# One-core decoder block: 128x128 transposes by TensorE, or 32x32 blocks by VectorE with DMA between the block positions

## The chip, the cores and the metric

The kernel runs on one core of a Trainium2 chip. A core has TensorE (PE, matmuls; PEld is its weight load), VectorE (DVE), ScalarE (ACT), GpSimd (POOL) and SyncE (SP, which here issues almost all DMAs). The metric is device microseconds of one execution, as the median of several runs. The numbers of single instructions come from one profiled execution.

## The reference, cut to what matters

One layer of a decoder, 256 tokens by 2048 channels, all in float32:

```python
h = rms_norm(x, mix_norm_g)
p = h @ w_in                      # split into the inputs of three head groups
y_lru = rg_lru_branch(...)        # 512 channels
y_ml  = mlstm_branch(...)         # 768 channels; the last step is  h * norm_g * silu(z)
y_mo  = moba_branch(...)          # 768 channels; the last step is  o * silu(z)
x = x + concat([y_lru, y_ml, y_mo]) @ w_out
hx, hm = rms_norm(x, xa_norm_g), rms_norm(mem, mem_norm_g)
q = hx @ wq;  k, v = split(hm @ wkv)          # 4 heads of 128, 256 memory tokens
x = x + (softmax(q @ k.T * s) @ v) @ wo
return rms_norm(x, final_norm_g)
```

A matmul on TensorE contracts over the partitions. What stands with tokens on the partitions (a gated branch, the residual, the probabilities) has to be turned, so that channels (or memory tokens) stand on the partitions, before it can be contracted over them.

## The kernel before, in words

All weights are streamed from memory in 172 chunks, and each float32 operand is cut into a high and a low part, so that a product is three matmuls. The chunks are numbered in the order of use. Those that matter here: z1 is 92 to 99, z2 is 100 to 107, out0 to out3 (the output projection, four groups of 512 columns) are 108 to 139 in eights, ck0, ck2, cq0, cq2 are 140 to 155 in fours, cv is 156 to 163 and wo0 to wo3 are 164 to 171.

The order on every engine is written out by hand (manual schedule): each engine runs its instructions strictly in the order in which the program emits them. The loop over chunks `i` (L1100 to L1124) emits, in this order: `split(i + 4)`, which makes the high part of chunk `i + 4` on ACT (L197) and its low part on DVE (L198, through the helper at L148); `load(i + 8)` on SP's queue (L172), which waits until the raw buffer of chunk `i + 4` is free, that is, until DVE has made its low part, since there are 4 raw buffers; `mm(i)`, the matmuls of chunk `i` on PE; and then one `step()`. There are 6 pairs of high and low buffers, so `split(i + 4)` also waits for the matmuls of chunk `i - 2`.

`step()` runs the generator at the head of a queue of side work up to its next `yield`. I call the call of `step()` after `mm(i)` "step i". `done(name, a)` puts work on the queue when a group of columns is complete. For the stretch that the change touches, the steps of the kernel before are:

- step 99: `gate_z` of z1; steps 100 to 102: the last of `mo_heads`, which writes `o` (buffer w1); step 103: `ml_y` multiplies `hh` by its gate; steps 104, 105, 106: it turns pairs of 128 channels by `to_channels` (four PE transposes into one PSUM bank, L739) and cuts them into high and low parts, the operands y2, y3, y4 (L754, L755).
- step 107: `gate_z` of z2; step 108: `mo_y(0, 1)` multiplies; step 109: it turns and makes y5 (`split_pair`, ACT at L239, DVE at L240); step 110: `mo_y(1, 3)` multiplies; steps 111 and 112: y6 and y7.
- out0 reads y0 in chunk 108, y1 in chunk 109 and so on to y7 in chunk 115. The operands y0 and y1 come from another branch, much earlier.
- `x1_evac(a, g)` at the end of each out group adds the residual (step 115, 123, 131, 139) and turns the sum in two steps after it (L858), which gives h0 to h7, the operands of cq0 and cq2. Between them lie `x1_load` (the residual, L843) and `mem_stats` (loads of the transposed memory, L222, and their squares on ACT, L401).
- step 155 to 159: `cq_evac(a, 2)`: queries, scores and softmax for two tiles of 128 tokens, then for each tile eight PE transposes of the probabilities (L916) and two ACT copies (L917) into `C["pT"]`. After chunk 163 `cv_out` copies the values out of PSUM on ACT and DVE (L926, L927) and multiplies them with `C["pT"]` (L932, L937); the wo chunks follow.

Buffers of the pool `wk` are named by tag (`big(5, ...)` is tag w5) and there is one of each: a new tile of a tag waits until all readers of the old one are done.

Of the kernel before, what the change touches and what calls it, by code (L numbers as in the profile page):

```python
# [105 lines left out]
def kernel(ctx: ExitStack, tc: tile.TileContext, xT, memT, x, mem, ws, vec_d, lw_d, fg_d, out):  # L106
    nc = tc.nc
# [19 lines left out]
    def ps():  # L127
        nps[0] += 1
        return psp.tile([128, 512], F32, tag="ps", name=f"ps{nps[0]}")
# [77 lines left out]
    def act_pair(which, j):  # L207

        a = acts.tile([128, 2, 2, 256], F32R, tag="y" if which in "ym" else "x", name=f"a_{which}{j}")
        act_all[which][j] = a  # L210
        act_hi[which][j], act_lo[which][j] = a[:, :, 0, :], a[:, :, 1, :]
        return act_hi[which][j], act_lo[which][j]
# [518 lines left out]
                S.activation(dst[:, t, d0:d0 + c1 - c0], a[t][:, c0:c1], AF.Silu, scale=rstd["x"][:, t:t + 1])  # L731
        yield

    def to_channels(src, c):

        p = ps()
        for cc in range(2):
            for t in range(2):
                P.transpose(p[:, cc * 256 + t * 128:cc * 256 + t * 128 + 128],  # L739
                            src[:, t, (c + cc) * 128:(c + cc) * 128 + 128], ident)  # L740
        return p

    def ml_y():
        hh, sz = M["h"], M["sz"]
        for t in range(2):
            tt(hh[:, t, :], hh[:, t, :], sz[:, t, :], OP.mult)
        yield
        for j in range(3):
            p = to_channels(hh, 2 * j)
            h, l = act_pair("y", 2 + j)  # L750
            for cc in range(2):
                sl = slice(cc * 256, cc * 256 + 256)
                ng = vc("ng", 2 * j + cc)
                S.activation(h[:, cc, :], p[:, sl], AF.Copy, scale=ng)  # L754
                stt(l[:, cc, :], p[:, sl], ng, h[:, cc, :].bitcast(F32), OP.mult, OP.subtract)  # L755
            yield


    B = {}
# [67 lines left out]
    def mo_y(j0, j1):  # L827
        o, sl = B["o"], slice(256 * j0, 256 * j1)
        for t in range(2):
            tt(o[:, t, sl], o[:, t, sl], B["sz"][:, t, sl], OP.mult)  # L830
        yield
        for j in range(j0, j1):
            split_pair("y", 5 + j, to_channels(o, 2 * j))
            yield


    X1 = {}
# [9 lines left out]
    def x1_evac(a, g):  # L847
        t1 = X1[g]
        for t in range(2):
            tt(t1[:, t, :], a[t], t1[:, t, :], OP.add)  # L850
            junk = small("yt", 512)
            S.activation(junk, t1[:, t, :], AF.Square, accum_out=ssq1[:, t, g:g + 1])
        yield
        for j in range(2):
            p = ps()
            for kk in range(2):
                for t in range(2):
                    P.transpose(p[:, kk * 256 + t * 128:kk * 256 + t * 128 + 128],  # L858
                                t1[:, t, (2 * j + kk) * 128:(2 * j + kk) * 128 + 128], ident)
            split_pair("h", 2 * g + j, p)  # L860
            yield

    def x1_rstd():
        r = small("rstd_1", 2)
# [14 lines left out]
    def cq_evac(a, c):  # L879
        if c == 0:  # L880
            C["q"] = big(2, 4, 256)
        qT = C["q"]
        fold(qT[:, c:c + 2, :], a)
        if c == 0:
            yield
            return
        sc, nsc = small("ca_sc", 2), small("ca_nsc", 2)
        V.tensor_scalar(sc, rstd["1"], DH_SCALE, None, op0=OP.mult)
        V.tensor_scalar(nsc, rstd["1"], -DH_SCALE, None, op0=OP.mult)
        yield  # L890
        pr = [big(6, 4, 256), big(9, 4, 256)]
        for t in range(2):
            mx, sm_ = small(f"ca_mx{t}", 4), small(f"ca_sm{t}", 4)
            for hp in range(2):
                p = ps()
                for hh_ in range(2):
                    h = 2 * hp + hh_
                    P.matmul(p[:, hh_ * 256:hh_ * 256 + 256], qT[:, h, t * 128:t * 128 + 128], C["k"][:, h, :],
                             start=True, stop=True)
                V.reduce_max(mx[:, 2 * hp:2 * hp + 2], p.rearrange("p (a b) -> p a b", a=2), axis=AX.X)  # L900
                V.tensor_scalar(mx[:, 2 * hp:2 * hp + 2], mx[:, 2 * hp:2 * hp + 2], nsc[:, t:t + 1], None, op0=OP.mult)
                for hh_ in range(2):
                    h = 2 * hp + hh_
                    S.activation(pr[t][:, h, :], p[:, hh_ * 256:hh_ * 256 + 256], AF.Exp, scale=sc[:, t:t + 1],
                                 bias=mx[:, h:h + 1], accum_out=sm_[:, h:h + 1])
            V.reciprocal(sm_, sm_)
            for h in range(4):
                V.tensor_scalar(pr[t][:, h, :], pr[t][:, h, :], sm_[:, h:h + 1], None, op0=OP.mult)
            yield
        C["pT"] = [big(2, 4, 2, 128), big(5, 4, 2, 128)]  # L910
        for t in range(2):
            for hp in range(2):
                p = ps()
                for i in range(4):
                    h, m = 2 * hp + i // 2, i % 2
                    P.transpose(p[:, i * 128:i * 128 + 128], pr[t][:, h, m * 128:m * 128 + 128], ident)  # L916
                S.activation(C["pT"][t][:, 2 * hp:2 * hp + 2, :, :].rearrange("p a b c -> p (a b c)"), p, AF.Copy)  # L917
            yield

    def c_pair(t):  # L920
# [1 line left out]
        return a[:, 0, :, :], a[:, 1, :, :]  # L922

    def cv_out(a):
        v = [wk.tile([128, 512], F32, tag=f"w{i}", name=f"cv{i}") for i in (6, 1)]
        S.activation(v[0], a[0], AF.Copy, scale=rstd["m"][:, 0:1])  # L926
        V.tensor_scalar(v[1], a[1], rstd["m"][:, 1:2], None, op0=OP.mult)  # L927
        C["oh"], C["ol"] = [], []
        pv = [ps(), ps()]
        for t in range(2):  # L930
            for h in range(4):
                P.matmul(pv[t][:, h * 128:h * 128 + 128], v[0][:, h * 128:h * 128 + 128], C["pT"][t][:, h, 0, :],  # L932
                         start=h == 0, stop=False, skip_group_check=True)
        for t in range(2):
            p = pv[t]
            for h in range(4):
                P.matmul(p[:, h * 128:h * 128 + 128], v[1][:, h * 128:h * 128 + 128], C["pT"][t][:, h, 1, :],  # L937
                         start=False, stop=True, skip_group_check=True)
            oh, ol = (v.rearrange("p a b -> p (a b)") for v in c_pair(t))
            S.activation(oh, p, AF.Copy)  # L940
            tt(ol, p, oh.bitcast(F32), OP.subtract)
            C["oh"].append(oh)
            C["ol"].append(ol)
# [50 lines left out]


    queue = deque()

    def bg(*gens):
        queue.extend(gens)
# [6 lines left out]

    def step(n=1):

        while queue and n > 0:
            try:  # L1010
                if next(queue[0]):
                    return
                n -= 1
            except StopIteration:
                queue.popleft()

    def drain():
        while queue:
            step()

    def idle(n):
# [173 lines left out]
```

## Time and profile before

| | |
|---|---|
| time, median of 3 runs | 522.26 us (521.66 to 522.65) |
| the profiled execution, its time | 521.88 us |
| the profiled execution, its span | 520.2 us |
| PE busy | 507.9 us |
| DVE busy | 338.0 us |
| ACT busy | 292.8 us |
| DMA moved | 98.74 MB, mean 190 GB/s |

The span is what the profile shows between the first and the last instruction; the 1.7 us between span and time lie around it. "Busy" is the time in which an engine has an instruction in work; issuing a DMA is not counted as busy. A wait in the trace is named after what ended it.

### The profile page before, as it was taken

The numbers are of one execution on the slowest core, as the hardware profiler recorded it, in microseconds if no ns is written. First come the engines' busy times: TensorE is split into PE (matmuls) and PEld (weight loads), VectorE is DVE, ScalarE is ACT, GpSimd is POOL, SyncE is SP. The second block draws the span as 40 slices with busy tenths as digits, with TensorE's granted clock in tenths as the row PEclk, the third lists the DMA queues.
The fourth block names the chain that finished last, engine by engine and source line by source line (L and its number), as shares of the span: only waits on it lengthen the run. The fifth ranks groups of instructions, "written<-read, shape, count | busy, mean of one in ns | idle before, by whom it ended". The sixth has DMA issues, their size and how long they took to land.

```text
span 520.2 us, 7578 instructions
## 1 busy us (share of the span) xinstructions
PE 507.9 (98%) x2814; PEld 448.8 (86%) x2814; DVE 338.0 (65%) x531; ACT 292.8 (56%) x476; POOL 54.8 (11%) x70
## 2 busy tenths in 40 slices
PE   8999999999999999999999999999999999999993
PEld 6999889998988888889988888888888888888883
DVE  5958848895397656548645466654658749637574
ACT  5775477678544333353545755543649467546353
POOL 2800001000132100002000000000132003000000
PEclk9999999999999999999999999999999999999998
DMA  8995635467446544435843465478575527734704
GB/s 274 360 412 180 187 120 167 139 221 230 160 160 178 186 161 163 151 92 183 271 155 121 137 209 179 164 272 325 188 264 174 194 66 259 237 128 129 234 3 161
DMA packets 31077, 98.74 MB, mean 190 GB/s; under 512 B 3520, under 2 KB 3904, under 8 KB 31040
## 3 DMA queue, kind: packets, MB, share of 16 engines
q1 hardware_dynamic: 30896, 98.25, 56.9%
q8 instruction: 22, 0.36, 0.3%
q14 instruction: 15, 0.12, 0.1%
q10 hardware_dynamic: 144, 0.01, 0.0%
HBM read 96.15 MB, written 2.10 MB: 189 GB/s over the span
## 4 chain that ended last, share of the span: by engine, by line
PE 85%; issue 6%; POOL 3%; DVE 3%; DMA 1%; ACT 1%; SPq 1%; POOLq 0%; ACTq 0%; DVEq 0%
PE acc_out L284 5%; PE acc_out L282 5%; PE acc_out L283 5%; PE acc_q L260 4%; PE acc_k L260 4%; PE acc_z L284 4%; PE acc_z L282 4%; PE acc_z L283 4%; PE acc_cq L260 3%; PE acc_lz L260 3%; PE acc_q L261 2%; PE acc_k L261 2%; PE acc_o L283 2%; PE acc_o L282 2%; PE acc_o L284 2%
## 5 line engine op out<-in xcount | busy, mean ns | idle before, releaser
L148 DVE TENSOR_TENSOR wl<-raw,wh 128x1024 fp32r<-128x1024 f32 (+3 forms) x166 | 199.6, 1212 | 111.7 <-ACT wh L197 109.3
L197 ACT ACTIVATE wh<-raw 128x1024 fp32r<-128x1024 f32 (+2 forms) x162 | 161.8, 1013 | 44.5 <-DMA raw<-ws 14.8
L282 PE MATMUL acc_out<-wh,a_y 128*128 128x512 f32 x128 | 50.8, 397 | 0.0
L284 PE MATMUL acc_out<-wh,a_y 128*128 128x512 f32 x128 | 49.9, 390 | 0.0
L283 PE MATMUL acc_out<-wl,a_y 128*128 128x512 f32 x128 | 49.8, 389 | 0.0
L282 PE MATMUL acc_z<-wh,a_x 128*128 128x512 f32 x96 | 39.6, 412 | 0.0
L284 PE MATMUL acc_z<-wh,a_x 128*128 128x512 f32 x96 | 37.6, 391 | 0.0
L283 PE MATMUL acc_z<-wl,a_x 128*128 128x512 f32 x96 | 37.5, 390 | 0.0
L260 PE MATMUL acc_k<-a_x,wh 128*128 128x512 f32 x96 | 34.4, 401 | 0.0
L260 PE MATMUL acc_q<-a_x,wh 128*128 128x512 f32 x96 | 34.1, 398 | 0.0
L451 POOL TENSOR_TENSOR w<-ev,rrow 128x512 f32<-128x512 f32 x11 | 17.5, 1589 | 153.6 <-DVE ev L148 153.6
L284 PEld LDWEIGHTS acc_out<-wh,a_y 128*128 128x128 f32 x128 | 24.0, 188 | 5.2
L283 PEld LDWEIGHTS acc_out<-wl,a_y 128*128 128x128 f32 x128 | 24.1, 188 | 4.7
L282 PEld LDWEIGHTS acc_out<-wh,a_y 128*128 128x128 f32 x128 | 24.1, 188 | 4.6
L261 PE MATMUL acc_k<-a_x,wl 128*128 128x256 f32 x96 | 26.9, 280 | 0.0
L261 PE MATMUL acc_q<-a_x,wl 128*128 128x256 f32 x96 | 26.8, 280 | 0.0
L402 POOL TENSOR_TENSOR mask<-mask,yt 128x512 f32<-128x512 f32 x7 | 10.3, 1473 | 147.1 <-ACT yt L401 147.1
L260 PE MATMUL acc_lz<-a_x,wh 128*128 128x512 f32 x64 | 23.3, 406 | 0.0
L260 PE MATMUL acc_ck<-a_m,wh 128*128 128x512 f32 x64 | 23.1, 403 | 0.0
L260 PE MATMUL acc_cq<-a_h,wh 128*128 128x512 f32 x64 | 22.7, 399 | 0.0
L283 PE MATMUL acc_o<-wl,a_x 128*128 128x392 f32 (+1 forms) x64 | 21.6, 338 | 0.0
L282 PE MATMUL acc_o<-wh,a_x 128*128 128x392 f32 (+1 forms) x64 | 21.6, 337 | 0.0
(302 smaller groups left out, 1187.4 us busy)
## 6 DMA issues: line engine op xcount, KB each, us to landing
raw<-ws SPq DMA_DIRECT2D x138, 512.0 KB, 4.1
raw<-ws SPq DMA_DIRECT2D x24, 384.0 KB, 3.1
w<-x SPq DMA_DIRECT2D x8, 512.0 KB, 6.5
raw<-ws SPq DMA_DIRECT2D x8, 392.0 KB, 3.1
w<-memT SPq DMA_DIRECT2D x8, 256.0 KB, 6.1
out<-xg SPq DMA_DIRECT2D x8, 256.0 KB, 3.0
w<-xT SPq DMA_DIRECT2D x7, 256.0 KB, 6.7
raw<-ws SPq DMA_DIRECT2D x4, 256.0 KB, 5.0
```

The costliest lines, as they stand in the source:

```text
L148: V.tensor_tensor(out, a, b, op)
L197: S.activation(h[:, :kc * n], r[:, :kc * n], AF.Copy)
L260: P.matmul(a[m], h[:, sl], both, start=first, stop=False, skip_group_check=True)
L261: P.matmul(a[m][:, :256], l[:, sl], xh, start=False, stop=last, skip_group_check=True)
L282: P.matmul(o, xh[:, sl], mh, start=first, stop=False)
L283: P.matmul(o, xh[:, sl], ml, start=False, stop=False)
L284: P.matmul(o, xl[:, sl], mh, start=False, stop=last)
L402: G.tensor_tensor(sq[which], sq[which], q, OP.add)
L451: G.tensor_tensor(dst, e, rb(which), OP.mult)
```

## The change

Three places that turned 128x128 tiles on PE now do it in two moves: one DVE instruction transposes every 32x32 block in place of its position (into a buffer `tmp`), and 16 DMAs from SBUF to SBUF carry block (i, j) to position (j, i) for all tiles at once. Each of the 16 DMAs has 32 partitions and one piece of 32 floats (128 bytes) per tile. `turn` is called nine times: for `ml_y` (12 tiles), `mo_y` (4 tiles, then 8), `x1_evac` (8 tiles, four times) and the probabilities (8 tiles, twice). What read the turned PSUM bank is put into a generator `finish` on a list `side`; every `step()` advances all of `side` first, and `finish` lets 4, 2 or 3 steps pass (`idle`) before it reads. ACT's copies at L917 are gone. In `cv_out` the first buffer of the values is now w2 in place of w6.

```diff
-    def to_channels(src, c):
-        p = ps()
-        for cc in range(2):
-            for t in range(2):
-                P.transpose(p[:, cc * 256 + t * 128:cc * 256 + t * 128 + 128],
-                            src[:, t, (c + cc) * 128:(c + cc) * 128 + 128], ident)
-        return p
+    def turn(dst, tmp, src):
+        V.transpose(tmp, src)
+        for i in range(4):
+            for j in range(4):
+                nc.sync.dma_start(dst[32 * j:32 * j + 32, :, 32 * i:32 * i + 32],
+                                  tmp[32 * i:32 * i + 32, :, 32 * j:32 * j + 32])
+
+    def blocks(t, c0, c1):
+        return t[:, :, c0 * 128:c1 * 128].rearrange("p t (c k) -> p c t k", k=128)

     def ml_y():
...
-        for j in range(3):
-            p = to_channels(hh, 2 * j)
-            h, l = act_pair("y", 2 + j)
...
+        tmp, hT = big(8, 6, 2, 128), big(4, 6, 2, 128)
+        turn(hT.rearrange("p a b c -> p (a b) c"), tmp.rearrange("p a b c -> p (a b) c"), blocks(hh, 0, 6))
+        def finish():
+            yield from idle(4)
+            for j in range(3):
+                h, l = act_pair("y", 2 + j)
...
+                yield
+        side.append(finish())
+        yield
...
     def mo_y(j0, j1):
...
-        yield
-        for j in range(j0, j1):
-            split_pair("y", 5 + j, to_channels(o, 2 * j))
-            yield
+        if j0 == 0:
+            B["tmp"], B["oT"] = big(5, 6, 2, 128), big(9, 6, 2, 128)
+        oT = B["oT"]
+        cs = slice(2 * j0, 2 * j1)
+        turn(oT[:, cs]..., B["tmp"][:, cs]..., blocks(o, 2 * j0, 2 * j1))
+        def finish():
+            yield from idle(2)
+            for j in range(j0, j1):
+                split_pair("y", 5 + j, oT[:, 2 * j:2 * j + 2].rearrange("p a b c -> p (a b c)"))
+                if j < 2:
+                    yield
+        side.append(finish())
+        yield
...
     def x1_evac(a, g):
...
-                    P.transpose(...)
-            split_pair("h", 2 * g + j, p)
-            yield
+        tmp, xT1 = big(1, 4, 2, 128), big(2, 4, 2, 128)
+        turn(xT1..., tmp..., blocks(t1, 0, 4))
+        def finish():
+            yield from idle(3)
+            for j in range(2):
+                split_pair("h", 2 * g + j, xT1[:, 2 * j:2 * j + 2].rearrange("p a b c -> p (a b c)"))
+                yield
+        side.append(finish())
+        yield
...
     def cq_evac(a, c):
...
-        C["pT"] = [big(2, 4, 2, 128), big(5, 4, 2, 128)]
-        for t in range(2):
-            for hp in range(2):
-                p = ps()
-                for i in range(4):
-                    h, m = 2 * hp + i // 2, i % 2
-                    P.transpose(p[:, i * 128:i * 128 + 128], pr[t][:, h, m * 128:m * 128 + 128], ident)
-                S.activation(C["pT"][t][:, 2 * hp:2 * hp + 2, :, :].rearrange("p a b c -> p (a b c)"), p, AF.Copy)
+        C["pT"] = []
+        for t in range(2):
+            tmp, pT = big(1 + t, 8, 128), big(5 + t, 8, 128)
+            turn(pT, tmp, pr[t].rearrange("p h (m k) -> p (h m) k", k=128))
+            C["pT"].append(pT.rearrange("p (h m) k -> p h m k", m=2))
             yield
...
     def cv_out(a):
-        v = [wk.tile([128, 512], F32, tag=f"w{i}", name=f"cv{i}") for i in (6, 1)]
+        v = [wk.tile([128, 512], F32, tag=f"w{i}", name=f"cv{i}") for i in (2, 1)]
...
     def step(n=1):
+        for g in list(side):
+            if next(g, True):
+                side.remove(g)
         while queue and n > 0:
...
     def drain():
-        while queue:
+        while queue or side:
             step()
```

## Rows read from the trace of the kernel before

**Rows 1.** The page, part 1: busy us (share of the span) xinstructions.
```profile
PE 507.9 (98%) x2814; PEld 448.8 (86%) x2814; DVE 338.0 (65%) x531; ACT 292.8 (56%) x476; POOL 54.8 (11%) x70
```
**Rows 2.** Busy time by stretch: bounds, length, PE, PEld, DVE, ACT, POOL; clock, DMA, GB/s.
```profile
294.00:320.00 26.00, 26.00 (x133) 21.87 (x132) 16.40 (x18) 18.02 (x32) 0.00 (x0) 1.00 0.55 182
```
**Rows 3.** Chain of waits: start us, us, what; the three kinds of transpose groups.
```profile
309.82 0.43 PE ps L739 x4
...
345.34 0.44 PE ps L858 x4
...
470.68 0.87 PE ps L916 x8
```
**Rows 4.** Timeline of SP's queue at the start: start us, us to issue, line, DMA.
```profile
1.23 0.42 SPq L169 DMA_DIRECT2D raw<-ws  x1
1.70 0.42 SPq L222 DMA_DIRECT2D w<-xT  x1
...
5.50 0.65 SPq L222 DMA_DIRECT2D w<-xT  x1
6.75 0.33 SPq L172 DMA_DIRECT2D raw<-ws  x1
```
**Rows 5.** DMA from 0 to 14 us: a queue's packets, MB, share; issues, us to landing.
```profile
q10 hardware_dynamic: 144, 0.01, 0.7%
...
w<-xT SPq DMA_DIRECT2D x2, 128.0 KB, 2.6
...
vec<-vec ACTq DMA_DIRECT2D x1, 8.0 KB, 2.2
```
**Rows 6.** Timeline of DVE, 300 to 350 us: start us, us, line, operation, out<-in [idle before].
```profile
308.88 1.22 DVE L148 TENSOR_TENSOR wl<-raw,wh 128x1024 fp32r<-128x1024 f32 x1
310.81 0.48 DVE L151 SCALAR_TENSOR_TENSOR a_y<-ps,vec,a_y 128x256 fp32r<-128x256 f32 x1 [0.71 <-ACT a_y L754]
...
325.93 0.69 DVE L148 TENSOR_TENSOR a_y<-ps,a_y 128x512 fp32r<-128x512 f32 x1 [1.65 <-ACT a_y L239]
...
328.02 1.29 DVE L148 TENSOR_TENSOR w<-w,w 128x512 f32<-128x512 f32 x2
```
**Rows 7.** Timeline of ACT, 300 to 350 us.
```profile
319.02 1.26 ACT L731 ACTIVATE w<-acc_z,rstd_x 128x512 f32<-128x512 f32 x2
320.16 2.01 ACT L197 ACTIVATE wh<-raw 128x1024 fp32r<-128x1024 f32 x2
325.30 0.60 ACT L239 ACTIVATE a_y<-ps 128x512 fp32r<-128x512 f32 x1 [3.13 <-PE ps L739]
```
**Rows 8.** Timeline of PE: first matmuls of chunks 108, 109 and 110 (out0).
```profile
319.22 0.39 PE L282 MATMUL acc_out<-wh,a_y 128*128 128x512 f32 x1
...
321.94 0.39 PE L282 MATMUL acc_out<-wh,a_y 128*128 128x512 f32 x1
...
325.02 0.48 PE L282 MATMUL acc_out<-wh,a_y 128*128 128x512 f32 x1
```
**Rows 9.** Waits of the whole span: who waited for whom, us in total, times, longest.
```profile
ACT yt L852 <- PE ps L433: 9.2, 1, 9.2
PE acc_ck L261 <- DVE wl L148: 0.8, 1, 0.8
```
**Rows 10.** Timeline of DVE at the softmax of the cross-attention.
```profile
462.64 0.69 DVE L900 TENSOR_REDUCE ca_mx<-ps 128x2 f32<-128x512 f32 x1 [1.06 <-PE ps L898]
...
474.35 1.22 DVE L148 TENSOR_TENSOR wl<-raw,wh 128x1024 fp32r<-128x1024 f32 x1
```
**Rows 11.** Timeline of ACT, at the copy of the values.
```profile
484.78 0.69 ACT L926 ACTIVATE cv<-acc_cv,rstd_m 128x512 f32<-128x512 f32 x1 [2.07 <-PE acc_cv L293]
```
**Rows 12.** Timeline of PE, probabilities times values.
```profile
485.94 1.95 PE L932 MATMUL ps<-w,cv 128*128 128x128 f32 x16
```
**Rows 13.** Busy time by stretch, as rows 2, around the last matmul.
```profile
511.00:512.00 1.00, 0.95 (x8) 0.74 (x7) 0.44 (x2) 0.51 (x2) 0.00 (x0) 1.00 0.00 0
516.00:517.00 1.00, 0.00 (x0) 0.00 (x0) 0.00 (x0) 0.00 (x0) 0.00 (x0) 0.67 1.09 342
```

More of the change, by code (lines that the diff above doesn't have):

```diff
@@ L747, in ml_y @@
         yield
-        for j in range(3):
-            p = to_channels(hh, 2 * j)
-            h, l = act_pair("y", 2 + j)
[L751 to L755, printed above, removed]
-            yield
+        tmp, hT = big(8, 6, 2, 128), big(4, 6, 2, 128)
[4 more added lines that the diff above has]
+                h, l = act_pair("y", 2 + j)
+                for cc in range(2):
+                    src = hT[:, 2 * j + cc, :, :].rearrange("p a b -> p (a b)")
+                    ng = vc("ng", 2 * j + cc)
+                    S.activation(h[:, cc, :], src, AF.Copy, scale=ng)
+                    stt(l[:, cc, :], src, ng, h[:, cc, :].bitcast(F32), OP.mult, OP.subtract)
+                yield
+        side.append(finish())
+        yield
     B = {}
@@ L830, in mo_y @@
             tt(o[:, t, sl], o[:, t, sl], B["sz"][:, t, sl], OP.mult)
+        if j0 == 0:
+            B["tmp"], B["oT"] = big(5, 6, 2, 128), big(9, 6, 2, 128)
+        oT = B["oT"]
+        cs = slice(2 * j0, 2 * j1)
+        turn(oT[:, cs].rearrange("p a b c -> p (a b) c"), B["tmp"][:, cs].rearrange("p a b c -> p (a b) c"),
+             blocks(o, 2 * j0, 2 * j1))
+        def finish():
[5 more added lines that the diff above has]
+        side.append(finish())
         yield
-        for j in range(j0, j1):
-            split_pair("y", 5 + j, to_channels(o, 2 * j))
-            yield
     X1 = {}
@@ L853, in x1_evac @@
         yield
-        for j in range(2):
-            p = ps()
-            for kk in range(2):
-                for t in range(2):
-                    P.transpose(p[:, kk * 256 + t * 128:kk * 256 + t * 128 + 128],
-                                t1[:, t, (2 * j + kk) * 128:(2 * j + kk) * 128 + 128], ident)
-            split_pair("h", 2 * g + j, p)
-            yield
+        tmp, xT1 = big(1, 4, 2, 128), big(2, 4, 2, 128)
+        turn(xT1.rearrange("p a b c -> p (a b) c"), tmp.rearrange("p a b c -> p (a b) c"), blocks(t1, 0, 4))
+        def finish():
[5 more added lines that the diff above has]
+        yield
     def x1_rstd():
@@ L909, in cq_evac @@
             yield
-        C["pT"] = [big(2, 4, 2, 128), big(5, 4, 2, 128)]
+        C["pT"] = []
         for t in range(2):
-            for hp in range(2):
-                p = ps()
-                for i in range(4):
-                    h, m = 2 * hp + i // 2, i % 2
-                    P.transpose(p[:, i * 128:i * 128 + 128], pr[t][:, h, m * 128:m * 128 + 128], ident)
-                S.activation(C["pT"][t][:, 2 * hp:2 * hp + 2, :, :].rearrange("p a b c -> p (a b c)"), p, AF.Copy)
+            tmp, pT = big(1 + t, 8, 128), big(5 + t, 8, 128)
+            turn(pT, tmp, pr[t].rearrange("p h (m k) -> p (h m) k", k=128))
+            C["pT"].append(pT.rearrange("p (h m) k -> p h m k", m=2))
             yield
@@ L996 @@
     queue = deque()
+    side = []
     def bg(*gens):
```

## The prediction

> **What bounds the kernel now.** I read the busy times first: PE is busy for 507.9 us of a span of 520.2 us, DVE and ACT for about two thirds and just over half of it [rows 1]. An average says little about a stage, so the stretch in which the change begins comes next: PE is busy for all of its 26 us [rows 2]. The chain of waits says the same from the other side: the PE transposes lie on it, 0.43 to 0.44 us for a group of four and 0.87 us for a group of eight [rows 3]. So PE's own instructions are the time, and whatever PE no longer does is saved in full, as long as nothing makes PE wait. SP issues a DMA every 0.47 us when it has several in a row (0.42 us each and a small gap [rows 4]); this interval, s below, decides the case.
>
> **What is removed.** There are 14 groups of four transposes (six at L739, eight at L858) and two groups of eight at L916: 14 x 0.44 + 2 x 0.87 = 7.9 us of PE [rows 3]. ACT's copies at L917 were off the path and count as nothing. A second, smaller gain: in the kernel before, ACT waits 9.2 us for a PE matmul of the memory statistics, and PE then loses 0.8 us for a low part in ck0 [rows 9]. The side list lets the queue move sooner, the statistics end in out2 (steps 129 and 130), and this wait should go: 0.8 us. Together -8.7 us.
>
> **What is added.** No row shows a DVE block transpose. The nearest are one-input and two-input DVE operations: 0.69 us for 512 elements per partition [rows 10], 1.22 us for 1024 [rows 6]; the line through them gives 1.8 us for 1536. I take these (at half the rate the times would double, which adds 1 to 2 us in each place below). The nine turns issue 144 DMAs on SP. For s, 0.47 us is the value at back-to-back issue; the ends are 0.33 us, the shortest issue, and 0.65 us, one that was held by an earlier DMA [rows 4]. The time from issue to landing is 2.2 to 2.6 us for the smallest transfers [rows 5]; I take 2.4 us.
>
> A DMA of the 12-tile turn moves 32 x 12 pieces of 128 bytes, 24 for each of 16 DMA engines. The nearest row is a queue of 144 packets, nearly all of 64 bytes, with 0.7% of 14 us x 16 engines: 11 ns each [rows 5]. At 11 ns per piece that is 0.26 us, at 22 ns (twice the bytes) 0.53 us; for 8 tiles 0.18 or 0.35 us. So the issue, not the movement, sets the pace: 16 x 0.47 = 7.5 us for a turn.
>
> The Trainium skill, "DMA: Bandwidth & Descriptors", section "Specifications", speaks against such pieces: below 512 bytes a transfer misses line rate, because of a read-modify-write. Its section "Why small descriptors are slow (HBM only)" exempts transfers inside SBUF. By the first the pieces would take about twice as long (the second rival below), by the second the sum here stands; no row of this trace shows an SBUF to SBUF transfer.
>
> **First place: y2 and y5 at out0.** All times are those of the trace before. The 12-tile turn is in step 104, behind the low part of chunk 108 on DVE, which ends at 310.1 [rows 6]; the transpose ends at 311.9. SP then issues 16 DMAs until 319.4, after that the load of chunk 113 (until 319.9), which stood behind them, and then the 16 DMAs of the 4-tile turn, which now comes in step 105: until 327.4, landed at 329.8. The reader of this turn, y5, is in step 108 and thus on ACT ahead of the high part of chunk 113 and of y2 (step 109). ACT gets there early: the gate of z2 follows PE, which is 1.3 us ahead by then, and with the high part of chunk 112 ACT is done at about 319.9 [rows 7]. It waits 9.9 us for the DMAs. Behind it on DVE are queued y5's low part, the gating for the second `mo_y`, its transpose, and the low part of chunk 113. So: ACT's copy 0.60 to 330.4 [rows 7], y5's low part 0.69, the product 1.29, the 8-tile transpose 1.22, chunk 113's low part 1.22, the first half of y2's low part 0.48 [rows 6]: 335.3.
>
> PE reads y2 in chunk 110. Before, that chunk began at 325.02, two chunks of 2.72 us and one transpose group after 319.22 [rows 8]; without the four groups before it PE is there at 323.2. It stands still for 12.1 us. After that y6 lands at 333.6 + 7.5 + 2.4 = 343.5, is ready at 344.8, and chunk 114 begins at 346.2: no second hold. Weights: the load of chunk 117 leaves SP only at 341.2, against its use at 354; covered.
>
> **Middle: the four turns of the residual.** Transposes end some 5 us after the last matmul of a group, the DMAs are issued 7.5 us later and landed at about 15 us; h0 stands in step 120, and ACT reaches it after about 10 us. ACT waits 5 us, and the weights that SP could not load meanwhile come as late. The high and low parts of a chunk run up to four chunks (11 us) ahead of PE, which takes this in. The memory loads of `mem_stats` now queue on SP behind the first turn and their squares hold ACT as well, to within 2 us of PE's use by my count. Bounds 0 and 4 us; I take 1 us, since the weights lead by more than the wait.
>
> **Tail: the probabilities.** The low part of chunk 162 ends at 475.6 on DVE [rows 10], the first transpose at 476.8, its DMAs are issued until 484.3; the load of chunk 167 stands between, and the second turn's DMAs leave until 492.3 and land at 494.7. `cv_out` copies the values into w2, which is the `tmp` of this second turn, so even the first product waits for it. The copy takes 0.69 us and PE starts 0.47 us after its end, as before [rows 11, 12]: 495.9. PE would be there at 485.94 - 1.74 = 484.2 [rows 3, 12]. Hold: 11.7 us. The load of chunk 168 leaves at about 492.8 and is used some 12 us after 495.9; covered.
>
> **The clock.** [...] No row shows how fast it rises again. [...] I take 2 us each, 4 us.
>
> **Sum.** 12.1 + 11.7 + 1.0 + 4.0 - 8.7 = +20.1 us on the profiled execution's 521.9 us: 542.0 us; that execution is 0.4 us under the median, so 542 us. Both holds have 32 issues ahead of them, so 0.1 us of s is 6.4 us of time: s = 0.33 gives 533 us, s = 0.65 gives 554 us.
>
> **The rivals.** *Cheap issue, on the other side.* If SP issues these small DMAs in under 0.22 us, the holds shrink by 64 x 0.25 = 16 us, PE idles too briefly for the clock, and the balance is not slower; at 0.1 us both holds are gone and the time is 521.9 - 8.7 + 1 = 514 us. For it: the DMAs are small. Against it: SP and ACT take 0.33 to 0.43 us for an issue whatever its size (128 to 512 KB), and none is shorter [rows 4]. Chance 0.06.
>
> *The pieces set the pace.* At 44 ns per piece (22 ns doubled) a DMA takes 1.06 us for 12 tiles and 0.70 us for 8. The first hold grows by 16 x 0.59 = 9.5 us, y6 comes another 2.4 us late, the tail grows by 2 x 3.8 = 7.6 us, and the middle by about 4 us: 565 us, and more if pieces are slower still. Chance 0.17.
>
> *Half the holds.* If ACT or the tail is less exposed than counted, because issue is near 0.33 us and the clock does not fall, or because one hold does not occur: 523 to 532 us. Chance 0.08.
>
> *The change does not do what it says*, so that PE still transposes: 522 us, chance 0.02.
>
> **How the numbers follow.** The forecast, 533 to 554 us, has 0.67. The range of 8 in 10 is 526 to 570 us: it leaves out the cheap issue, the unchanged case, a part of the half-hold case and the far part of the slow pieces. This kernel's runs agree to about 0.2%, some 1 us. Faster 0.06, within 0.2% 0.03, slower 0.91.
>
> **What would show it.** Right: no PE transposes at the three lines, nine DVE transposes, 144 more issues on SP at 0.47 us; a PE gap of about 12 us ahead of the third chunk of out0 that ends with y2's low part, with ACT's wait for a DMA just before it at y5; a second gap of about 12 us before the first product of probabilities and values, behind ACT's copy of the values, which waits for a DMA; a granted clock of 0.5 behind each gap. Wrong: issues under 0.25 us, landings that come much later than the issues, or PE gaps in the four out groups.

## The result, and the profile after

The changed kernel takes 576.32 us (575.13 to 577.58), the kernel before, run beside it, 522.45 us (521.66 to 522.76): a ratio of 1.103, 95% interval 1.100 to 1.106. The direction was predicted; the size, +53.9 us against a forecast of +20, was not, and the time lies outside the range of 526 to 570 us.

The page of the changed kernel, the lines that answer to [rows 1] and the shares of the chain of waits:

```profile
span 573.5 us, 7646 instructions
PE 511.7 (89%) x2742; PEld 449.0 (78%) x2742; DVE 347.5 (61%) x540; ACT 291.3 (51%) x472; POOL 55.2 (10%) x70
...
PE 58%; SPq 15%; issue 9%; DMA 6%; DVE 5%; ACT 3%; POOL 2%; ACTq 0%; POOLq 0%; DVEq 0%
```

PE issues 72 instructions fewer and is busy for 3.8 us longer, since part of its work runs at a lower clock; it now stands idle for 62 us. SP's queue, which issues DMAs, is on the chain with 15%. The added instructions, by line (ns: shortest, median, longest), and two lines of the page's DMA issues (KB each, us to landing):

```profile
L737 DVE STREAM_TRANSPOSE w<-w x9: 711/1240/1770, 311.1 to 514.0; 128x1024 f32<-128x1024 f32 x7, 128x1536 f32<-128x1536 f32 x1, 128x512 f32<-128x512 f32 x1
...
L740 SPq DMA_DIRECT2D w<-w x144: 585/609/1263, 313.0 to 533.9; - x144
...
w<-w SPq DMA_DIRECT2D x112, 32.0 KB, 2.0
...
w<-w SPq DMA_DIRECT2D x16, 48.0 KB, 2.1
```

DVE's transposes take 0.71, 1.24 and 1.77 us for 512, 1024 and 1536 elements. The DMAs land after 2.0 us, the larger ones hardly later; but each issue takes 0.61 us.

The first hold, at out0. Timelines of SP, ACT, DVE and PE (start us, us, ..., in brackets the idle time before and its releaser):

```profile
312.99 10.68 SPq L740 DMA_DIRECT2D w<-w  x16
323.76 0.55 SPq L172 DMA_DIRECT2D raw<-ws  x1
324.42 10.24 SPq L740 DMA_DIRECT2D w<-w  x16
334.76 1.48 SPq L172 DMA_DIRECT2D raw<-ws  x3
...
336.12 0.63 ACT L239 ACTIVATE a_y<-w 128x512 fp32r<-128x512 f32 x1 [15.33 <-DMA w<-w]
...
336.78 0.69 DVE L148 TENSOR_TENSOR a_y<-w,a_y 128x512 fp32r<-128x512 f32 x1 [14.74 <-ACT a_y L239]
...
338.14 0.80 PE L282 MATMUL acc_out<-wh,a_y 128*128 128x512 f32 x1 [13.60 <-ACT a_y L762]
...
341.51 0.79 PE L284 MATMUL acc_out<-wh,a_y 128*128 128x512 f32 x1 [2.15 <-DVE a_y L151]
```

Compare [rows 7, 8]: ACT now stands at y5 for 15.3 us, and y2, queued behind it, lets PE wait 13.6 us for its high part and 2.1 us more for its low part. Both turns together keep SP from 313.0 to 334.7, 21.7 us for 33 issues: 0.66 us each.

The middle (the residual's turns), and the tail:

```profile
369.17 11.16 SPq L740 DMA_DIRECT2D w<-w  x16
380.44 0.54 SPq L172 DMA_DIRECT2D raw<-ws  x1
381.02 0.43 SPq L222 DMA_DIRECT2D w<-memT  x1
...
385.12 0.63 ACT L401 ACTIVATE yt<-w 128x512 f32<-128x512 f32 x1 [13.61 <-DMA w<-memT]
...
536.06 0.69 ACT L949 ACTIVATE cv<-acc_cv,rstd_m 128x512 f32<-128x512 f32 x1 [7.46 <-DMA w<-w]
...
536.80 3.78 PE L955 MATMUL ps<-w,cv 128*128 128x128 f32 x16 [16.32 <-ACT cv L949]
```

In the middle, a weight and a load of the memory stand behind 16 issues on SP, and ACT waits 13.6 us for that load, with the high parts of the weights queued behind it. In the tail, PE waits 16.3 us for ACT's copy of the values, and that copy waits for the DMAs of the second turn, which read from the buffer that it is to write. The 16 matmuls behind that wait take 3.78 us against 1.95 before [rows 12]. PE's waits over the whole span (us in total, times, longest), then the clock around the first hold:

```profile
PE ps L955 <- ACT cv L949: 16.3, 1, 16.3
PE acc_out L282 <- ACT a_y L762: 13.6, 1, 13.6
PE ps L433 <- DVE yt L430: 11.9, 2, 10.9
PE acc_out L282 <- ACT wh L197: 4.6, 1, 4.6
PE acc_out L284 <- DVE a_y L151: 2.1, 1, 2.1
```
```profile
310.00:320.00 10.00, 10.00 (x46) 8.29 (x45) 7.64 (x9) 3.67 (x5) 0.00 (x0) 1.00 0.54 136
320.00:330.00 10.00, 4.54 (x21) 3.42 (x19) 1.23 (x1) 0.78 (x1) 0.00 (x0) 0.84 0.51 100
330.00:340.00 10.00, 1.22 (x2) 0.50 (x2) 3.19 (x5) 3.88 (x7) 0.00 (x0) 0.50 0.50 158
...
341.50:347.20 5.70, 5.69 (x13) 4.46 (x14) 4.21 (x7) 0.48 (x2) 0.00 (x0) 0.50 0.28 43
347.20:350.00 2.80, 2.80 (x13) 2.26 (x12) 0.00 (x0) 0.00 (x0) 0.00 (x0) 0.99 0.36 53
```

The clock (the column behind POOL's) falls to 0.50, the lower level of 1.2 GHz, while PE is idle, as it fell behind the last matmul of the kernel before [rows 13]. Here PE still runs at that level after it has restarted at 338.1, until 347.2.

### The profile page after: what moved, and what is told of

The parts are those of the page before. It is cut to its first block, busy times and chain, and to the rows that moved or that the text cites. A ratio compares the mean times of both kernels' runs of the same rounds, so it can differ in the third digit from the quotient of the medians.

```text
span 573.5 us, 7646 instructions
## 1 busy us (share of the span) xinstructions
PE 511.7 (89%) x2742; PEld 449.0 (78%) x2742; DVE 347.5 (61%) x540; ACT 291.3 (51%) x472; POOL 55.2 (10%) x70
## 4 chain that ended last, share of the span: by engine, by line
PE 58%; SPq 15%; issue 9%; DMA 6%; DVE 5%; ACT 3%; POOL 2%; ACTq 0%; POOLq 0%; DVEq 0%
SPq L740 13%; PE acc_q L260 4%; PE acc_k L260 4%; PE acc_z L284 4%; PE acc_z L282 4%; PE acc_z L283 4%; DMA raw<-ws 3%; PE acc_lz L260 3%; PE acc_cq L260 2%; PE acc_k L261 2%; PE acc_o L283 2%; PE acc_q L261 2%; PE acc_o L282 2%; PE acc_o L284 2%; PE acc_v L284 2%
## 5 line engine op out<-in xcount | busy, mean ns | idle before, releaser
L282 PE MATMUL acc_out<-wh,a_y 128*128 128x512 f32 x128 | 53.4, 417 | 18.2 <-ACT a_y L762 13.6
L284 PE MATMUL acc_out<-wh,a_y 128*128 128x512 f32 x128 | 52.5, 410 | 2.1 <-DVE a_y L151 2.1
L283 PE MATMUL acc_out<-wl,a_y 128*128 128x512 f32 x128 | 52.6, 411 | 0.7 <-DVE wl L148 0.7
L282 PEld LDWEIGHTS acc_out<-wh,a_y 128*128 128x128 f32 x128 | 25.9, 202 | 24.6 <-ACT a_y L762 14.0
L284 PEld LDWEIGHTS acc_out<-wh,a_y 128*128 128x128 f32 x128 | 25.5, 200 | 8.3 <-DVE a_y L151 2.9
L283 PEld LDWEIGHTS acc_out<-wl,a_y 128*128 128x128 f32 x128 | 25.7, 201 | 6.9 <-DVE wl L148 1.2
L402 POOL TENSOR_TENSOR mask<-mask,yt 128x512 f32<-128x512 f32 x7 | 11.2, 1600 | 146.9 <-DVE wl L148 123.8
L260 PE MATMUL acc_cq<-a_h,wh 128*128 128x512 f32 x64 | 22.8, 400 | 1.2 <-ACT wh L194 1.2
```

The lines of the kernel that those rows point to most:

```text
L260: P.matmul(a[m], h[:, sl], both, start=first, stop=False, skip_group_check=True)
L282: P.matmul(o, xh[:, sl], mh, start=first, stop=False)
L283: P.matmul(o, xh[:, sl], ml, start=False, stop=False)
L284: P.matmul(o, xl[:, sl], mh, start=False, stop=last)
L402: G.tensor_tensor(sq[which], sq[which], q, OP.add)
```

## The experiments

**One part at a time.** Three kernels each keep one place of the change and leave the other two on PE as before. e2: `ml_y` and `mo_y` turned by DVE and DMA. e3: only `x1_evac`. e4: only the probabilities.

```diff
 def x1_evac(a, g):          # e2 and e4: as in the kernel before
-        turn(xT1..., tmp..., blocks(t1, 0, 4))
+        P.transpose(...) into ps(), split_pair("h", ..., p)
```

> Only the gated branches are turned by blocks and DMA; the residual and the probabilities are turned on PE as before. From the changed kernel's trace: PE does 15 matmuls (3.4 us of work) between 324.4 and 347.2 us, so the hold at the third chunk of out0, with the lower clock behind it, costs 19.4 us, less six transpose groups of 0.44 us. Theory (each turn is 16 issues of 0.655 us in a row on one queue, and the reader of the second turn stands ahead of the reader of the first on ACT): +16.8 us, about 539 us. Rival (the holds come from the DMA traffic of all nine turns together): under 530 us.

Measured: 539.69 us, 1.033 (1.031 to 1.035) of 522.75.

> Only the residual is turned by blocks and DMA. In the changed kernel the four out groups lose about 18 us in two holds, one at a weight chunk of out1 (4.6 us) and one at the statistics matmul of out2 (10.9 us), each with the lower clock behind it. Theory 'collision': both holds exist because memory loads and statistics, moved earlier by the gated branches' shorter queue, meet a turn; alone, the four turns hold ACT but PE little: -3.5 us for eight transpose groups, -0.8 us for the old wait in ck0, +1 to +5 us of holds: 519 to 524 us. Rival 'each turn costs by itself': +15 us or more, about 537 to 540 us.

Measured: 541.29 us, 1.037 (1.035 to 1.038).

> Only the cross-attention's probabilities are turned by blocks and DMA. In the changed kernel the first product of probabilities and values waits 16.3 us and runs at the lower clock, some 2.6 us more, less 1.7 us of transposes. Theory: this hold does not depend on the other turns: +17.2 us, about 539.6 us. Rival (it is mostly inherited from the delays before it): under 530 us. The parts of this run, of the run with the branches alone and of the run with the residual alone then add up to less than the change's 54 us; what is missing is what they cost each other.

Measured: 539.86 us, 1.033 (1.032 to 1.035).

The parts give +16.9, +18.5 and +17.1 us, in sum 52.6 of the 53.9: three losses of about the same size that add up. The two holds were read rightly from the trace; the collision that I had expected to explain the middle (loads and statistics moved earlier by the branches' turns) was not its cause, since the residual's turns cost as much alone. Where they cost it, in e3 (ACT's timeline, PE's waits):

```profile
396.75 0.63 ACT L401 ACTIVATE yt<-w 128x512 f32<-128x512 f32 x1 [14.56 <-DMA w<-memT]
```
```profile
PE acc_out L282 <- ACT wh L197: 8.8, 2, 8.0
PE ps L433 <- DVE yt L430: 6.3, 2, 5.7
```

The load of the memory is late, then the weights' high parts behind it on ACT, then the memory's statistics.

**What makes an issue slow.** e1 and e7 are the kernel before with sets of DMAs added at its end, where nothing else uses SP's queue; only the rows of these DMAs matter. The forms in short (read `x`, an input, for memory; bsrc and dst lie in SBUF):

```diff
+    f_sp:      dst[32j:32j+32, :, 32i:32i+32]  <- bsrc[32i:32i+32, :, 32j:32j+32]   # e1 L1151; on ACT's queue L1173
+    f_whole:   dst[32j:32j+32, 2i:2i+2, :]     <- bsrc[32i:32i+32, 2j:2j+2, :]      # e1 L1157
+    f_packed:  as f_whole, read in 8 pieces                                         # e1 L1163
+    f_wide:    dst[:, :, 32i:32i+32]  <- bsrc[:, :, 32i:32i+32], 128 partitions     # e1 L1168
+    f_run:     dst[:, i, :] <- bsrc[:, i, :]             # e7 L1150, SBUF to SBUF, 128 partitions
+    f_lane:    the same on 32 partitions                 # e7 L1154
+    f_in32:    32 partitions, one run, from memory       # e7 L1158
+    f_in32p:   32 partitions, 8 pieces, from memory      # e7 L1162
+    f_in128:   128 partitions, from memory               # e7 L1167
```

> The kernel before, with five sets of SBUF to SBUF DMAs added behind its last output, only to read the time that the queue takes to issue each form (the added work is not part of the computation). In the changed kernel one issue took 0.61 us and the next came 0.655 us after it, where 0.47 us had been forecast. Forms: 32 partitions with 8 pieces of 128 bytes on both sides (as in the change); 32 partitions with 1 KB in one run on both sides; pieces on the source side only; 128 partitions with 8 pieces (4 DMAs); the first form from ACT's queue. Theory 'pieces': the issue is dearer because both sides have a third dimension of short pieces, so the first, the fourth and the fifth take about 0.61 us, one run on both sides takes 0.42 us, the one-sided form lies between. Rival 'few partitions': all forms with 32 partitions take 0.61 us and the one with 128 takes 0.43 us. Rival 'traffic': the queue is held by other loads in the changed kernel; then all forms take 0.43 us here, where nothing else moves.

```profile
L1151 SPq DMA_DIRECT2D w<-w x16: 585/622/860, 516.7 to 528.1; - x16
...
L1157 SPq DMA_DIRECT2D w<-w x16: 588/589/606, 529.0 to 538.5; - x16
...
L1163 SPq DMA_DIRECT2D w<-w x16: 608/609/633, 539.1 to 548.9; - x16
...
L1168 SPq DMA_DIRECT2D w<-w x4: 677/684/765, 549.6 to 551.8; - x4
...
L1173 ACTq DMA_DIRECT2D w<-w x16: 593/623/802, 516.3 to 527.4; - x16
```

All three theories fell: whole runs of 1 KB take 0.59 us as the pieces do, at the end of the kernel as in its middle, ACT's queue is no faster, and four times the partitions (L1168) cost 0.07 us more. The sets of L1151 and L1173 ran side by side, though: SP and ACT together issued 32 DMAs in about 12 us, where SP alone takes 10 us for 16. What all of these share is that both ends lie in SBUF, so e7 sets that against loads from memory:

> The kernel before, again with sets of DMAs behind its last output only to read issue times (not part of the computation). The first set of forms left neither the pieces nor the 32 partitions as the cause: 32 partitions with one run of 1 KB from SBUF to SBUF still took 0.59 us to issue, 128 partitions with 8 pieces 0.68 us. New forms: SBUF to SBUF, 128 partitions, one run of 512 bytes; the same on 32 partitions that keep their place; memory to SBUF on 32 partitions, one run; memory to SBUF on 32 partitions with 8 pieces of 128 bytes; memory to SBUF on 128 partitions, one run. Theory 'both ends in SBUF': the first two take about 0.59 us, the last three 0.33 to 0.45 us. Rival 'short transfers and few partitions': the forms with 32 partitions take 0.6 us from memory too.

```profile
L1150 SPq DMA_DIRECT2D w<-w x8: 557/600/606, 516.1 to 520.6; - x8
...
L1154 SPq DMA_DIRECT2D w<-w x8: 588/589/597, 521.2 to 525.6; - x8
...
L1158 SPq DMA_DIRECT2D w<-x x8: 415/420/577, 526.3 to 529.7; - x8
...
L1162 SPq DMA_DIRECT2D w<-x x4: 422/448/449, 530.2 to 531.6; - x4
```

From memory an issue takes 0.42 to 0.45 us, with one run or 8 pieces on 32 partitions, or one run on 128 (L1167, 0.43); from SBUF to SBUF 0.59 to 0.60 us. Where a DMA has many more pieces, their number counts as well: 128 partitions with 8 pieces each took 0.68 us (L1168), and e10 below shows it for reads from memory. By the first and last starts the intervals are 3.4 / 7 = 0.49 and 1.4 / 3 = 0.47 us against 4.5 / 7 = 0.64 and 4.4 / 7 = 0.63 us. The prediction's 0.47 us came from loads from memory.

**The same blocks by way of memory.** e10 turns at all three places, but writes the blocks to device memory with 4 DMAs and reads them back with 4.

```diff
-        for i in range(4):
-            for j in range(4):
-                nc.sync.dma_start(dst[32j...], tmp[32i...])
+        for i in range(4):
+            nc.sync.dma_start(d[i]..., tmp[32i:32i+32]...)
+        for i in range(4):
+            nc.sync.dma_start(dst[:, :, 32i:32i+32], d[i]...)
```

> The changed kernel with the 16 DMAs of a turn replaced by 8 by way of device memory: 4 write the transposed blocks out, 4 read them back in place; the 128-byte pieces stay on the reading side, and as many bytes move twice. Theory (the number of issues on the queue sets the time): a turn takes the queue for 8 x 0.47 us and one landing of about 2.2 us in between, 6 us against 10.5 us, and is landed after 8.4 us against 12.5 us; where two turns stand in a row, at out0 and in the tail, each hold shrinks by about 8 us and the middle ones by half or more: about 541 us (533 to 550). Rival (the small pieces and the traffic set the time): no gain or a loss against 576 us, since the bytes move twice.

Measured: 547.3 us, 1.050 (1.047 to 1.053), 29 us less than the changed kernel. The first turn holds SP from 312.44 to 319.35 (lines below), 6.9 us against 10.7, though its data move twice. So the issues, and not the bytes, set the pace. They are not all alike: the writes (L749) take 0.43 to 0.47 us each in the median, but the reads (L752), with 128 partitions in pieces of 128 bytes, 0.61 us for 8 tiles and 1.00 us for 12, among the kernel's other traffic.

```profile
312.44 2.39 SPq L749 DMA_DIRECT2D turnB<-w  x4
315.02 4.33 SPq L752 DMA_DIRECT2D w<-turnB  x4
```

**y5 behind y2.** e5 is the changed kernel with `idle(5 if j0 == 0 else 2)` in `mo_y`, so that ACT makes y2 before it waits for y5.

> The changed kernel with one number altered: the reader of the first mo_y turn lets 5 steps pass, not 2, so that y2, y3 and y4 stand ahead of y5 on ACT. Theory (the hold at out0 is 40 issues of 0.655 us in a row before y6, in whatever order they are read): y2 comes some 8 us sooner, but then PE waits for y6 in its fifth chunk, which the third turn lands at about 347.5 us of the changed kernel's time; gain 6 us, about 570 us. Rival (the order on ACT alone makes the hold: y5 ahead of y2): the hold at y2 and its second half (2.1 us) shrink by more than 10 us and the clock stays up: gain 14 to 17 us, 559 to 562 us.

Measured: 572.7 us, 1.098 (1.095 to 1.101) of 521.51: +51.2 us against +53.9, about 3 us less than the changed kernel, with intervals that just touch. PE's longest waits for a y operand are now 5.7 and 5.0 us in place of 13.6, but it waits 6.8 us for a high part of weights. The order on ACT is worth little, because the next operand and the weights stand behind the same issues.

**The middle, one neighbour after the other.** All of these turn only the residual, except e6. e8 keeps SP's queue and lets the reader come 6 steps after the turn (in place of 3), with the squares and statistics of the memory later too.

```diff
-            yield from idle(3)
+            yield from idle(6)          # x1_evac; in mem_stats square("m", j - 5), and 4 steps between the halves of stats("m")
```

> Only the residual is turned by blocks and DMA (541.3 us with the change's spacing, against 522.7 us), but what reads late data is moved later: the squares of the memory come 5 steps after their load, not 2, h0 to h7 are read 6 steps after the turn, not 3, and four steps pass between the two halves of the memory statistics. Theory (the holds come from ACT, DVE and PE standing in order in front of data whose DMA is queued behind 10.5 us of issues; the turn's length itself is harmless if nobody waits for it): all holds go, 8 x 0.44 + 0.8 us are saved: about 518.5 us (517.5 to 521). Rival (the queue being taken for 10.5 us starves the weight loads, whoever reads what): holds of several us stay, 528 us or more.

Measured: 545.12 us, 1.045 (1.043 to 1.047). No reader waits for the turn now, but a weight does, behind the first turn:

```profile
362.62 1.06 ACT L197 ACTIVATE wh<-raw 128x1024 fp32r<-128x1024 f32 x1 [10.94 <-DMA raw<-ws]
...
392.43 1.06 ACT L197 ACTIVATE wh<-raw 128x1024 fp32r<-128x1024 f32 x1 [11.04 <-DMA raw<-ws]
```

The first of these waits costs PE next to nothing; behind the second turn it is as long, and there PE waits 4.1 us. PE also waits 8.7 us for the squares, which my own spacing had probably made late (argued, no run separates it), and 3.4 us for a high part in cq0. e6 is the changed kernel with `nc.gpsimd.dma_start` in `turn`; e11 is e8's residual with that and without the later squares; e12 is e11's spacing with e10's way through memory on SP.

> The changed kernel with all 144 DMAs of the turns issued from GpSimd's queue instead of SP's, so that no weight load, residual load or memory load stands behind them. Theory 'the queue is taken': what the middle lost (18.5 us with only the residual turned) is the weights and the memory that SP could not load; it falls to at most 4 us, while the two holds at out0 and at the probabilities stay, because their readers wait for 32 issues in a row on any one queue. If GpSimd issues as fast as SP (0.65 us), that is 576 - 15 = 561 us (556 to 566). Theory 'the turn's own latency': the readers of the turn (h0 to h7) wait for the landing and not for weights; then the middle keeps its loss and the time is 576 us or more. No run has shown yet what an issue costs on GpSimd: each 0.1 us more than SP's moves the two holds by 6.4 us together, which is to be read from the two holds (19.4 and 16.3 us in the changed kernel) and not from the total. Signs: ACT's longest wait for a weight load under 4 us for the first theory, near 11 us for the second.

Measured: 580.08 us, 1.111 (1.109 to 1.113) of 521.88. GpSimd is no faster (0.58 us per issue, with gaps), and its DMAs land later: after 3.7 us in the median here and 5.6 us in e11 and e13, against 2.0 us from SP. ACT's longest wait for a weight is 2.8 us, so the weights are free, but the time is not less: the two holds grow (16.4 and 17.5 us in place of 13.6 and 16.3), and PE waits 12.3 us for the sum of squares that GpSimd makes behind its issues (`PE ps L426 <- POOL mask L404: 12.3, 1, 12.3`).

> Only the residual is turned by DVE and DMA (the heads' branches and the probabilities stay on PE as before); the 16 DMAs of each turn leave from GpSimd's queue, and the reader lets 6 steps (16 us) pass instead of 3. Theory 'the queue is taken' (SP's 10.5 us per turn starve the weights): without it the time is that of before less 8 transpose groups of 0.44 us, 522.3 - 3.5 = 519 us (518 to 523, the upper end if the squares of the memory, which are on GpSimd behind the issues, make the statistics late). Rival 'latency of the turn': 535 us or more, as in the same kernel with SP's queue (541.3 and, spaced by 6 steps, 545.1).

Measured: 544.99 us, 1.045 (1.043 to 1.046). As in e6, weights are at most 2.9 us late, and the loss has moved to GpSimd's own work. PE's timeline:

```profile
392.53 0.79 PE L282 MATMUL acc_out<-wh,a_y 128*128 128x512 f32 x1 [8.53 <-ACT wh L197]
...
425.06 1.19 PE L433 MATMUL ps<-yt,ones 128*128 128x256 f32 x2 [12.87 <-DVE yt L430]
```

The first is ACT held for 14.3 us by a sum on GpSimd, the second the power of the memory's statistics, which GpSimd began at 423.7, after the third turn.

> Only the residual is turned; each turn is 8 DMAs of SP's queue by way of device memory (4 out, 4 back), which took SP 6 to 7 us per turn in the run where all turns went that way, against 10.5 us for 16 DMAs inside SBUF; the reader lets 6 steps pass. Theory 'the queue is taken': the weights lead PE by up to four chunks (11 us) and are loaded 4 us late at most, so most of the loss goes: 520 to 529 us. Rival 'latency of the turn': the way through memory is longer than inside SBUF, so the time is at least that of the SP turn, 541 us or more.

Measured: 533.96 us, 1.024 (1.022 to 1.026): between the two theories' times. With SP taken for 5.8 to 6.5 us by each of the first two turns PE still waits 5.8 us for the statistics and 3.7 us for a high part.

e13 takes GpSimd's other work out of e11's way: the sums of squares go to DVE (`V.tensor_tensor`), the statistics come two steps earlier.

> As the run before it (only the residual is turned, the 16 DMAs of each turn leave from GpSimd's queue, the reader lets 6 steps pass), with GpSimd's other work taken out of the way: the sums of the memory's squares are made by DVE (0.69 us each, seven) and the memory's statistics come two steps earlier, so that their power on GpSimd stands ahead of the third turn and not behind it. In the run before, weights were never late by more than 2.9 us, and PE lost 8.5 us for a high part behind ACT's 14.3 us wait for a sum on GpSimd, and 12.9 us for that power. Theory 'whatever shares the issuing engine waits for 16 issues': with nothing urgent behind the turns both holds go, and what is left is the gain, 8 transpose groups of 0.44 us: 521.9 - 3.5 = 518.5 us (517.5 to 521), faster than the kernel before. Rival 'the turns themselves cost' (their DMAs land late among the weights' traffic, or DVE's added work is late): h0 or h2 becomes the late operand, 525 us or more, with ACT's wait at the split of the turned residual on a DMA and PE's wait on a_h.

Measured: 540.25 us, 1.036 (1.033 to 1.038). The hold by the sums is gone; the power still stood behind the third turn, and PE's wait of 15.2 us ends with it (GpSimd's timeline, PE's waits). DVE had its input ready at 405.96, so 8.3 us of the wait are GpSimd's issues; the rest lies before that:

```profile
409.58 4.66 POOL L750 DMA_DIRECT2D w<-w  x8 [0.25 <-issue]
414.25 0.74 POOL L359 TENSOR_TENSOR rstd_m<-rstd_m,half 128x2 f32<-128x2 f32 x1
```
```profile
PE ps L433 <- DVE yt L430: 15.2, 1, 15.2
PE ps L426 <- DVE mask L404: 2.4, 1, 2.4
```

e14 moves the power ahead of the third turn, by loading the residual of groups 1 to 3 in one step; e15 puts the statistics one step later than e14, with GpSimd's order unchanged; e16 is the kernel before, PE's transposes and all, with e15's rearrangement of loads, squares and statistics.

```diff
-            bg(mo_y(1, 3), x1_load(0), x1_load(1), x1_load(2), x1_load(3), mem_stats())
+            bg(mo_y(1, 3), x1_load(0), x1_loads(), mem_stats())
...
-        yield from idle(2)          # ahead of stats("m"); e14: nothing, e15 and e16: idle(1)
```

> As the run before it, with the loads of the residual for groups 1 to 3 in one step instead of three, so that the memory's statistics come two steps earlier again and their power stands ahead of the third turn on GpSimd (in the run before it still stood behind it, and PE lost 15.2 us for it, the only hold over 2.4 us that was left in the middle). Theory 'whatever shares the issuing engine waits for 16 issues': that hold goes as well, and the turns of the residual cost nothing: 540.3 - 15.2 - 2.4 - 4 of clock = 518.7 us (517.5 to 521), against 522.3 of the kernel before. Rival 'the turns themselves cost': another hold of 5 us or more takes its place (h0 or h2 late behind the DMAs' landing, or a weight), 525 us or more.

Measured: 526.95 us, 1.011 (1.009 to 1.012).

> As the run before it, with the memory's statistics one step (2.7 us) later: there they came so early that PE waited 5.8 us for the last sum of squares, which waits for the memory's last load. GpSimd's order stays (the power ahead of the third turn). Theory 'whatever shares the issuing engine waits for 16 issues, and nothing else costs': the hold shrinks from 5.8 to about 3 us and is too short for the clock to fall much: 526.95 - 2.7 - 1 to 2 of clock = 522.5 to 523.5 us; without any hold it would be 518.5, so what is left is the hold itself. Rival 'the turns themselves cost': 526 us or more, with a hold that ends with a_h or with a weight.

Measured: 532.59 us, 1.020 (1.018 to 1.022).

> The kernel before, with TensorE's transposes, and with the rearrangement of the memory's statistics as in the run before it and nothing else: sums of squares on DVE, the residual's loads for three groups in one step, the statistics one step earlier. It tells what of that run's time belongs to the rearrangement. If the rearrangement costs nothing by itself: 521.5 to 522.5 us (0.8 us less where the kernel before waits for a low part behind the statistics). If it is the reason why that run is no faster than the kernel before: 524 us or more, with PE's wait for the sum of squares here too.

Measured: 520.82 us, 0.999 (0.998 to 1.000). PE's waits in e14, then in e15:

```profile
PE ps L426 <- DVE mask L404: 5.8, 1, 5.8
...
PE acc_cq L260 <- DVE a_h L148: 1.0, 1, 1.0
```
```profile
PE ps L426 <- DVE mask L404: 4.8, 1, 4.8
PE acc_cq L260 <- DVE a_h L148: 4.1, 2, 2.2
PE ps L433 <- DVE yt L430: 1.0, 1, 1.0
```

e14 loses 5 us where e3 lost 18.5, with the same 64 DMAs, from GpSimd's queue: 13 us of the middle was work queued behind the issues and, in e3, a reader that came early (ACT waits 22.0 us in three waits for the turned residual there, against 9.2 us in e14). The rest did not go. In e15 the memory's last load left SP 1.4 us later than in e14 (379.63 against 378.23), which is likely why the wait for the squares hardly shrank, and the turned residual itself became late for cq0 (4.1 us in two waits): the rival that the turns cost by themselves holds to that extent. The control shows no such wait and is no slower than the kernel before, so it is not the rearrangement. Of the 6.8 us by which e15's profiled span is longer than e14's (532.1 against 525.2), 3.0 us are idle time of PE and 3.8 us are its work, 510.8 us busy against 507.0: the granted clock was below 1.00 behind the squares in both (0.50 from 390 to 395 in e15), and in e15 again behind the waits in cq0 (0.88 from 460 to 465). What made the operands of e15 late was not settled; nor was a version found in which any of the turns pays.

## Why the prediction was right and wrong

*Right.* PE bounds the kernel, its 7.9 us of transposes are removed, and holds outweigh them. Both holds stand where the steps put them: the third chunk of out0, with y5 ahead of y2 on ACT, and the values, whose copy waits for the reused buffer. Neither place is the whole cause. e5 takes y5 out of y2's way and gains about 3 us, since the issues stay; and the products of the second tile need the second turn itself, whatever buffer the values go to (this is read from the kernel, no run tried it). The wait of 0.8 us [rows 9] went too, but e16 loses it without any turn. DVE's transposes (0.69, 1.22, 1.8 us assumed; 0.71, 1.24, 1.77 measured) and the landing (2.4 assumed, 2.0 measured) were sized well.

*The pieces.* The second rival's 565 us was nearer to the result than the forecast, for a reason that does not hold: pieces of 128 bytes land after 2.0 us and whole runs after 1.8 us (e1, L1151 and L1157), and whole runs are issued no faster. The Trainium skill, "DMA: Bandwidth & Descriptors", exempts transfers inside SBUF from its rule on small pieces ("Why small descriptors are slow (HBM only)"); the landings here agree.

*Failed: the interval s between issues.* I took 0.47 us from [rows 4], which are loads from memory, as the value for any DMA, and had 0.65 us only as an end. SBUF to SBUF it is 0.64 to 0.67 us in the two holds. By the prediction's own rule, 0.19 us more for 64 issues is 12 us; it had 554 us for that end. The measured excess in the two holds is of that size: heads +16.9 against 12.1 + 2 - 2.6 = +11.5, tail +17.1 against 11.7 + 2 - 1.7 = +12.0, together 10.5 us more. But not all of it is s: PE's waits grew by 3.6 us (15.7 against 12.1) and 4.6 us (16.3 against 11.7), 8.2 us together, and the rest is the clock, below.

*Failed: the middle.* It stood at 1.0 us, with bounds 0 and 4; with its saving of 3.5 us and the 0.8 us wait that was to go, the part came to -3.3 us, and it measured +18.5. This is 21.8 of the 34 us. The neighbours were seen (weights, memory loads and squares queued behind the turn) but each was held against the 11 us by which the weights lead, as if only one of them used it up. With 10.5 us per turn in place of 7.5 that lead is gone by the first neighbour: the load of the memory, counted as "within 2 us of PE's use", kept ACT 14.6 us in e3 and so the high parts behind it, and then the statistics. e8, e11, e13 and e14 free one neighbour each, and in each the next one appears.

*Failed: the clock.* The sum has 2 us for each of two holds, a price that no row of the kernel before shows. In the first one PE loses 19.4 us between 324.4 and 347.2 (22.8 us for 15 matmuls of 0.23 us), of which its two waits are 15.7; the other 3.7 us is work at the lower level, which lasts until 347.2, 9 us after the restart. In the tail it is 2.5 us (6.0 us from the first product to the first matmul of wo, against 3.5 before). The middle has such stretches too, for which the sum had none.

*The sum again, from the changed kernel's trace.* PE waits 15.7 us at out0 (12.1 in the sum), 16.3 at the values (11.7) and 18.4 in the middle (1.0). PE was busy for 507.9 us before, 500.0 without the transposes, and is now busy for 511.7; by this estimate the lower clock costs 11.7 us (4.0 in the sum). Less 7.9 for the transposes and the old wait of 0.8, that is 53.4 us, and the spans differ by 53.3. So the middle's waits are about half of what the forecast lacked, and s and the clock share the other half.

## What to carry to other kernels

An issue has to be priced from a row of the same kind of transfer; where the trace has none, the whole forecast belongs at the upper end, above all where the number is multiplied by 64. Replacing work on the bounding engine by many small DMAs moves the cost to the queue that issues them, so list everything else on that queue (loads, sums, statistics) and ask of each who waits for it; one lead of a few chunks covers only one of them. Moving the issues to another engine moves the list, it does not shorten it: fewer issues do. A split of one turn between SP's and ACT's queue is left open; e1 shows only that the two issue side by side.

## What the runs showed of the hardware

- Issue of a DMA on SP: 0.42 to 0.45 us from memory to SBUF in e7, 0.59 to 0.62 us from SBUF to SBUF (32 partitions in whole runs or pieces, 128 partitions in one run). With 128 partitions in pieces of 128 bytes it was 0.68 us inside SBUF (e1) and 0.61 to 1.00 us from memory (e10).
- SBUF to SBUF, ACT's queue took 0.62 us per issue with SP issuing beside it, 32 DMAs in about 12 us. GpSimd's took 0.58 us with gaps, and landed after 3.7 to 5.6 us in the median.
- A turn of 16 such DMAs costs 10.2 to 11.2 us of SP's queue, against a landing of 2.0 us.
- After a hold of PE the granted clock stayed at its lower level (0.50) while PE was already at work again, from 338.1 to 347.2 us at out0.
